# Clearing a kernel's semaphores from ScalarE beside the last store, instead of at the close of the context

## The chip, the cores and the metric

One core of a Trainium2 chip runs the kernel. In the trace each of its engines (TensorE, VectorE, ScalarE, GpSimd and SyncE) has records of its own, and these name the semaphores, which are shared counters, that an instruction waits for or counts: in the kernel before, VectorE waits for ScalarE seven times, 85.9 us in all, and ScalarE for loads five times, 34.7 us. The metric is device time in microseconds (us) of one execution. Each kernel but that of experiment 8 (fetch10) was executed several times, and the median is given with the lowest and highest run. Beside the time there is a profile of one execution; its span runs from the first to the last instruction and leaves out what comes before and after, so it is shorter than the time of the same execution: 162.18 us for 163.96 in the kernel before.

## The reference

The kernel computes log-sum-exp over the last axis of a float32 array of shape (32, 512, 1024):

```python
x_max = np.max(x, axis=axis, keepdims=True)
return (x_max.squeeze(axis) + np.log(np.sum(np.exp(x - x_max), axis=axis))).astype(np.float32)
```

That is 16,384 rows of 1,024 numbers, 67.11 MB to read and 64 KB to write. The kernel leaves out the maximum, which these inputs allow.

## The kernel before

Each of 128 partitions has 128 rows, loaded in 17 chunks into a ring of 51 rows. A chunk is a pair: its rows, and how many of them VectorE sums (ScalarE then takes only their exponentials; it sums the others itself, one row per instruction). The parts that matter here, with cuts marked:

```python
CHUNKS = [
    (4, 1), (15, 11), (16, 10), (16, 15), (16, 0), (14, 0), (12, 9), (9, 5), (7, 5), (5, 4),
    (4, 3), (3, 0), (2, 2), (2, 2), (1, 0), (1, 0), (1, 0),
]
# ...
    landed = [tc.alloc_semaphore(f"landed{i}") for i in range(len(CHUNKS))]
    act_done = tc.alloc_semaphore("act_done")
    dve_done = tc.alloc_semaphore("dve_done")
    stored = tc.alloc_semaphore("stored")
# ... loads on SyncE, exponentials on ScalarE, sums on VectorE or ScalarE ...
    take_logs(logged, NB, dves, acts)
    nc.scalar.wait_ge(act_done, acts)
    nc.scalar.dma_start(out=out_v, in_=res).then_inc(stored, 16)
    nc.gpsimd.wait_ge(stored, 16)
```

`tc` is the tile context. Semaphores taken from it are cleared when it closes. In the trace of this kernel the closing block that it writes holds a barrier over all five engines, then a clear of semaphores 99 to 118 by GpSimd (139 ns), then a second barrier. A barrier is: four engines report (each with an instruction called drain, which here adds one to semaphore 96), GpSimd takes the four reports, GpSimd releases (by semaphore 97), the four pass. From GpSimd's drain to the end of TensorE's record the first lasts 0.267 us (161.388 to 161.655) and the second 0.261 (161.918 to 162.179).

The softmax here doesn't subtract the row's maximum and nothing guards it: scores larger than these inputs give would overflow.

## Time and profile before

| | before |
|---|---|
| time, first three runs | 164.2 us (164.1 to 164.22) |
| time, all 33 runs of this study | 163.87 to 164.56 us, mean 164.16, standard deviation 0.18 |
| span of the profiled run | 162.18 us |
| issue of the store | 159.643 us |
| last of the store's 16 counts | 161.215 us |
| from that count to the end of the span | 0.964 us |

The prediction below shows the page's lines and reads them.

### The profile page before, as it was taken

Reading aid. Unit: us, or ns where it says so; the run is one execution under the profiler, and the core shown is the slowest. Engines: PE = TensorE matmul, PEld = TensorE weight load, DVE = VectorE, ACT = ScalarE, POOL = GpSimd, SP = SyncE. Lnnn points to the kernel's source line nnn. Section 1 sums busy time; section 2 is a strip of 40 time slices with the busy share of each in tenths; the row PEclk is TensorE's granted clock in tenths of the full one; section 3 lists DMA queues with packets and bytes.
Section 4 is the critical chain, followed back from the end, with each engine's and each line's share of the span. In section 5 each row is a group of like instructions: output and inputs, shape, how many; then the busy total and the mean of one; then the engine's idle time right before and its main releaser. Section 6 shows DMA issues by size and latency. Waiting matters only on the chain.

```text
span 162.2 us, 213 instructions
## 1 busy us (share of the span) xinstructions
DVE 72.9 (45%) x11; ACT 124.1 (76%) x136; POOL 0.2 (0%) x4
## 2 busy tenths in 40 slices
DVE  0030000039960799000999900000006999799591
ACT  3180006997099971999339999999999999999993
POOL 0000000000000000000000000000000000000000
DMA  6999899969969959969988999999999999999970
GB/s 263 497 485 470 349 394 517 485 291 517 485 291 517 517 259 517 517 275 501 517 368 370 424 424 432 461 497 388 436 427 399 431 400 439 420 424 414 415 318 16
DMA packets 2593, 67.18 MB, mean 414 GB/s; under 512 B 288, under 2 KB 416, under 8 KB 800
## 3 DMA queue, kind: packets, MB, share of 16 engines
q1 hardware_dynamic: 2448, 67.11, 96.4%
q10 hardware_dynamic: 144, 0.07, 0.1%
q14 instruction: 1, 0.01, 0.0%
HBM read 67.11 MB, written 0.07 MB: 414 GB/s over the span
## 4 chain that ended last, share of the span: by engine, by line
ACT 52%; DMA 38%; DVE 7%; issue 1%
DMA ring<-in_x_dram 38%; ACT ring L128 30%; ACT ring L116 22%; DVE sums L121 7%; ACT res L93 0%
## 5 line engine op out<-in xcount | busy, mean ns | idle before, releaser
L121 DVE TENSOR_REDUCE sums<-ring 128x5 f32<-128x5120 f32 (+8 forms) x11 | 72.9, 6648 | 86.0 <-ACT ring L116 85.9
L116 ACT ACTIVATE ring<-ring 128x5120 f32<-128x5120 f32 (+8 forms) x11 | 59.3, 5394 | 29.4 <-DMA ring<-in_x_dram 29.4
L128 ACT ACTIVATE ring<-ring 128x1024 f32<-128x1024 f32 x61 | 63.4, 1041 | 5.3 <-DMA ring<-in_x_dram 5.3
L128 ACT ACTIVATION_READ_ACCUMULATOR ring<-ring 128x1 f32 x61 | 11.4, 187 | 0.0
L103 ACT ACT_TABLE_LOAD x1 | 1.3, 1283 | 0.8 <-PEq L175 0.8
L93 ACT ACTIVATE res<-sums 128x67 f32<-128x67 f32 (+1 forms) x2 | 0.5, 256 | 0.1
L175 POOL MEMSET const-bfloat16-1.0<- 128x1 bf16 x1 | 0.1, 101 | 0.0
L175 POOL MEMSET const-uint8-127<- 128x1 uint8 x1 | 0.1, 101 | 0.0
L175 POOL MEMSET const-float32-0.0<- 128x1 f32 x1 | 0.1, 98 | 0.2 <-issue 0.2
L175 POOL MEMSET const-float32-1.0<- 128x1 f32 x1 | 0.1, 98 | 0.0
## 6 DMA issues: line engine op xcount, KB each, us to landing
ring<-in_x_dram SPq DMA_DIRECT2D x1, 7680.0 KB, 24.8
ring<-in_x_dram SPq DMA_DIRECT2D x1, 7168.0 KB, 36.1
ring<-in_x_dram SPq DMA_DIRECT2D x1, 6144.0 KB, 21.6
ring<-in_x_dram SPq DMA_DIRECT2D x1, 4608.0 KB, 32.1
ring<-in_x_dram SPq DMA_DIRECT2D x2, 2048.0 KB, 26.3
ring<-in_x_dram SPq DMA_DIRECT2D x1, 3584.0 KB, 40.2
ring<-in_x_dram SPq DMA_DIRECT2D x1, 2560.0 KB, 44.4
ring<-in_x_dram SPq DMA_DIRECT2D x2, 1024.0 KB, 46.0
```

The costliest lines, as they stand in the source:

```text
L93: nc.scalar.activation(out=res[:, lo:hi], in_=sums[:, lo:hi], func=Ln).then_inc(act_done, 1)
L103: nc.scalar.preload_act_table_set("natural_log_exp_and_others")
L116: nc.scalar.activation(out=ring[:, s : s + n_dve], in_=ring[:, s : s + n_dve], func=Exp).then_inc(act_done, 1)
L121: nc.vector.reduce_sum(out=sums[:, row : row + n_dve], in_=ring[:, s : s + n_dve], axis=AX).then_inc(dve_done, 1)
L128: nc.scalar.activation(out=ring[:, s + j], in_=ring[:, s + j], func=Exp, accum_out=sums[:, row + j : row + j + 1],).then_inc(act_done, 1)
L175: nc = _bacc.Bacc("TRN2", target_bir_lowering=False, num_devices=1)
```

## The change

The intent is to take the clear out of the ending. The semaphores now belong to the program and not to the context, so the context has nothing to clear; ScalarE clears them while the store is in flight, and GpSimd takes the store's own count back as it waits for it. The list of parts for the first load had one entry and goes away. Core of the diff:

```diff
-    landed = [tc.alloc_semaphore(f"landed{i}") for i in range(len(CHUNKS))]
-    act_done = tc.alloc_semaphore("act_done")
-    dve_done = tc.alloc_semaphore("dve_done")
-    stored = tc.alloc_semaphore("stored")
+    landed = [nc.alloc_semaphore(f"landed{i}") for i in range(len(CHUNKS))]
+    act_done = nc.alloc_semaphore("act_done")
+    dve_done = nc.alloc_semaphore("dve_done")
+    stored = nc.alloc_semaphore("stored")
+    used = sorted(sem.num for sem in [*landed, act_done, dve_done])
# ... the first load without its list of parts ...
     nc.scalar.dma_start(out=out_v, in_=res).then_inc(stored, 16)
+    nc.scalar.sem_clear(range(used[0], used[-1] + 1))
     nc.gpsimd.wait_ge(stored, 16)
+    nc.gpsimd.sem_inc(stored, -16)
```

More of the change, by code (lines that the diff above doesn't have):

```diff
@@ L16 @@
 LN_AT = 5
-FIRST_PARTS = [("sync", 0, 128)]
 @with_exitstack
@@ L50 @@
     res = nc.alloc_sbuf_tensor("res", [P, NB], fp32).ap()
-    landed = [tc.alloc_semaphore(f"landed{i}") for i in range(len(CHUNKS))]
-    act_done = tc.alloc_semaphore("act_done")
-    dve_done = tc.alloc_semaphore("dve_done")
-    stored = tc.alloc_semaphore("stored")
+    landed = [nc.alloc_semaphore(f"landed{i}") for i in range(len(CHUNKS))]
[3 more added lines that the diff above has]
+    used = sorted(sem.num for sem in [*landed, act_done, dve_done])
+    assert used == list(range(used[0], used[0] + len(used)))
     hook = nc.pop_inst_callback()
@@ L83, in load @@
             nc.sync.wait_ge(act_done, act_wait)
-        for engine, lo, hi in FIRST_PARTS if i == 0 else [("sync", 0, P)]:
-            getattr(nc, engine).dma_start(
-                out=ring[lo:hi, s : s + r], in_=x_v[lo:hi, row : row + r]
-            ).then_inc(landed[i], 16)
+        nc.sync.dma_start(out=ring[:, s : s + r], in_=x_v[:, row : row + r]).then_inc(
+            landed[i], 16
+        )
     def take_logs(lo, hi, dve_wait, act_wait):
@@ L113 @@
             take_logs(0, logged, *done_before[i])
-        nc.scalar.wait_ge(landed[i], 16 * (len(FIRST_PARTS) if i == 0 else 1))
+        nc.scalar.wait_ge(landed[i], 16)
         if n_dve:
```

## The prediction

> **What bounds the kernel now.** I began with the page's busy shares, its slices and the chain of waits, to see whether anything in the body can move. The kernel streams 67.11 MB from HBM through one ring of SBUF; ScalarE takes exponentials (alone or with an accumulated sum), VectorE sums part of the rows.
>
> ```profile
> DVE 72.9 (45%) x11; ACT 124.1 (76%) x136; POOL 0.2 (0%) x4
> DMA  6999899969969959969988999999999999999970
> q1 hardware_dynamic: 2448, 67.11, 96.4%
> ACT 52%; DMA 38%; DVE 7%; issue 1%
> ```
>
> The DMA row stands at 9 or 8 in most slices and the load queue holds 96.4% of the span of 16 engines: the body is bound by the transfer of x. ScalarE is full only in the second half, where it works off the chunks that have piled up in the ring. The chain alternates between loads (38%) and ScalarE (52%). GpSimd does 0.2 us of work and is in no link. The change touches neither the loads, nor an activation, nor a reduction, so the next view is the timeline of the last microseconds:
>
> ```profile
> 159.36 0.25 ACT L93 ACTIVATE res<-sums 128x61 f32<-128x61 f32 x1
> 159.64 0.37 ACTq L140 DMA_DIRECT2D out_dram<-res  x1
> ```
>
> The last logarithm ends at 159.61, the store is issued at 159.64, and the span ends at 162.18 (162.2 on the page). So 2.5 us lie after the last arithmetic. The issues view says that the 64 KB store lands 1.6 us after its issue, at 161.2. The rest, about 0.95 us, is neither compute nor data. Asking the trace for the line that closes the kernel (189, where all instructions made at the end of the context are put down) shows it:
>
> ```profile
> L189 POOLq EVENT_SEMAPHORE  x4: 17/17/17, 161.5 to 162.1; - x4
> L189 POOLq DRAIN  x3: 34/41/83, 161.4 to 161.9; - x3
> L189 POOLq COMPARE_BRANCH  x1: 33/33/33, 161.2 to 161.2; - x1
> L189 POOLq EVENT_SEMAPHORE_RANGE_CLEAR  x1: 139/139/139, 161.7 to 161.7; - x1
> ```
>
> The columns are engine, operation, count, duration in ns (least, median, most), and first and last start in us. GpSimd carries the ending. Its records in order of time, start in us and duration in ns, from the trace itself:
>
> ```
> 159.643  369  ScalarE  issue of the store
> 160.052  152  ScalarE  drain, ready for the first barrier
> 161.215       the 16th count of the store arrives
> 161.239   33  GpSimd   branch to the closing block (it holds the wait for the store)
> 161.388   41  GpSimd   drain                      }
> 161.473   17  GpSimd   takes the four arrivals    } first barrier
> 161.551   17  GpSimd   releases the four          }
> 161.604   51  TensorE  last engine passes
> 161.632   83  GpSimd   drain of the reset         } clear
> 161.744  139  GpSimd   semaphores 99 to 118 := 0  }
> 161.918   34  GpSimd   drain                      }
> 161.996   17  GpSimd   takes the four arrivals    } second barrier
> 162.074   17  GpSimd   releases the four          }
> 162.128   51  TensorE  last engine passes; the span ends at 162.179
> ```
>
> [...] the two event instructions last 17 ns each, but start 78 ns apart. So I count spacings from start to start. [...] Here, on ScalarE's queue, 64 KB at the page's mean of 414 GB/s would be 0.16 us, and 1.6 us pass[...]. That waiting time is the shadow the change wants to use. [...] semaphore 2 counts from 162.41 to 162.94, nearly all semaphores are written from 162.83 to 163.50, semaphore 2 counts again to 164.08. The profiled run took 163.96 us against a span of 162.18, so some 1.8 us are outside the kernel[...]. I take this part as unchanged.
>
> **The change part by part.**
>
> (a) The semaphores no longer belong to the tile context, so at its end the context has nothing of the kernel's to clear. Removed for certain, as I read it: the reset drain and the range clear. Without them the next GpSimd drain would start at 161.632 instead of 161.918: **0.286 us** less, all on the path, as nothing else runs then. What I must guess is whether the context then also leaves out the second barrier. That barrier exists to keep anyone from running on before the clear is done; with no clear it has no purpose. If it goes, the span ends as the last engine passes the first barrier, 161.604 + 0.051 = 161.655, and 162.179 - 161.655 = **0.524 us** go. I take this as the main case, with about 65%.
>
> (b) ScalarE clears 19 semaphores (17 landings, two counters) after issuing the store. Sized by GpSimd's clear: 139 ns, 222 with a reset drain. It starts at about 160.05, when the issue is over, so ScalarE's drain is over at about 160.204 + 0.222 = 160.43. GpSimd takes the arrivals at 161.473 in the kernel before. Over 1.0 us of slack: **0 us** on the path. Nothing still counts on these semaphores: the last wait of ScalarE asked for all activations and the one before it for all reductions.
>
> (c) GpSimd subtracts 16 as its wait is met. Before, the wait rode on the branch; now it should ride on one event instruction with the subtraction, ahead of the branch. Such an instruction costs GpSimd one spacing of 78 ns: **+0.08 us**, right on the path. If wait and subtraction were separate instructions it would be about 0.16.
>
> (d) The first load was already one transfer on SyncE; the list that could split it had one entry. Its removal changes no instruction: **0 us**.
>
> Sum of the main case: -0.524 + 0.078 = -0.45 us, 164.20 - 0.45 = 163.75 us, 0.27% less.
>
> **Rivals.** First, the second barrier stays and only the clear leaves the end: -0.286 + 0.078 = -0.21, so 163.99 us. For it: the kernel's text does not ask for a barrier less; against it: its lack of purpose. I give it 22%. Second, the clear merely changes its place, or the fixed part after the kernel absorbs the gain [...]: 164.2 to 164.3. Against it: in the trace that part starts 0.23 us after the last TensorE record, so it looks chained to the kernel's end. About 6%. Third, both barriers go and GpSimd's wait alone ends the kernel: then the path ends some 0.15 us after 161.239 + 0.078, near 161.47, and the saving is about 0.7 us, 163.5 us in all. For it: nothing but the wait is needed; against it: a context's end joins the engines whatever the semaphores. About 6%. Fourth, the clear on ScalarE becomes the wait that ends last: it would have to take over 1.0 us where GpSimd's took 0.139; 1%. No engine can become the bound, since none gets work before the store is issued.
>
> **Range and chances.** The weighted mean is near 163.8 us, and I put the prediction there, a little above the main case. The three timed runs before spread over 0.12 us; another chip or a slightly different supply of data may shift the median by as much again. All cases but the extremes lie in 163.45 to 164.15. Two per cent are 3.3 us. Everything that lies after the store's issue is 2.5 us in the trace, and most of that is the store itself, so faster by over 2% cannot come out of this; slower would need a delay of the loads for which the change has no cause. Within 2%: 0.98.
>
> **What would show it.** In the trace after: ScalarE's range clear on the line of the new clear, started near 160.05, while the store is in flight (step b); no range clear on GpSimd (a); the count of GpSimd's closing event instructions falls from 4 to 3, two for one barrier and one for the wait with the subtraction, if the second barrier went, and is 5 if it stayed; the stretch from the store's last count to the end of the span falls from 0.96 to about 0.52 us, or to about 0.76 in the first rival; start-to-start spacing of 0.08 us between the new wait and the branch (c). Up to 159.64 both traces should agree within the scatter of the loads, a few tenths of a us. The prediction is wrong if the body shifts by more than the tail saves, if the closing block keeps its shape, or if the part after the span grows as the span shrinks.

-0.524 for the clear and the second barrier, 0 for (b) and (d) and +0.078 for (c) come to -0.45 us, so to 163.75, and the mean weighted with the rivals to the 163.8 us that was predicted.

## More of the kernel before

One more line matters later, from the page's list of DMA queues (queue, kind, packets, MB, share of 16 engines' span):

```profile
q14 instruction: 1, 0.01, 0.0%
```

One transfer in the whole span does not carry data: 8 KB of instructions, at 89.05 us, 309 ns long.

## The result, and the profile after

| | before | changed |
|---|---|---|
| time, median of 6 runs each | 164.21 us (163.94 to 164.43) | 164.16 us (163.89 to 164.3) |
| span of the profiled run | 162.18 us | 162.45 us |
| sixth chunk (14 rows) landed | 100.647 us | 101.170 us |
| issue of the store | 159.643 us | 160.167 us |
| last of the store's 16 counts | 161.215 us | 161.747 us |
| from that count to the end of the span | 0.964 us | 0.701 us |

The ratio is 0.9995, with a 95% interval of 0.9981 to 1.0008. A ratio is the mean time of one kernel's runs over that of the other's runs of the same rounds, so it is not quite the ratio of the medians. In microseconds the interval says: between 0.31 less and 0.13 more. The whole kernel shows no difference; the two profiles show two, of opposite sign.

**The ending is 0.263 us shorter.** The view of the line that holds the closing block, in the changed kernel (engine, operation, count; duration in ns, least, median, most; first and last start in us):

```profile
L192 POOLq EVENT_SEMAPHORE  x4: 17/17/17, 161.9 to 162.3; - x4
L192 ACTq DRAIN  x2: 8/8/8, 160.7 to 162.2; - x2
L192 POOLq DRAIN  x2: 34/38/41, 161.9 to 162.1; - x2
```

And the views of the two new lines, ScalarE's clear and GpSimd's wait:

```profile
L142 ACTq EVENT_SEMAPHORE_RANGE_CLEAR  x1: 119/119/119, 160.6 to 160.6; - x1
L144 POOLq EVENT_SEMAPHORE  x1: 17/17/17, 161.8 to 161.8; - x1
```

Read the counts. GpSimd's closing block still has four event instructions, two per barrier, and the new wait is a fifth on a line of its own. So **both barriers stayed**; the reset drain, the range clear and the branch that carried the wait are gone from GpSimd. Following GpSimd's records from start to start shows where the time went:

| stretch (us) | before | changed |
|---|---|---|
| last count of the store, to GpSimd going on | 0.024 | 0.025 |
| GpSimd's wait, to its first drain | 0.149 | 0.080 |
| first drain, to the first release | 0.163 | 0.164 |
| first release, to the taking of the second four reports | 0.445 | 0.249 |
| that, to the second release | 0.078 | 0.078 |
| second release, to the end of the span | 0.105 | 0.105 |
| sum | 0.964 | 0.701 |

Two rows changed, by 0.069 and 0.196.

**The body was 0.52 us longer.** The chain of waits in order of time (start, duration, what), before:

```profile
47.15 36.52 DMA ring<-in_x_dram
83.69 10.55 ACT ring L128 x21
...
100.46 0.26 ACT res L93
100.72 14.60 ACT ring L128 x28
```

and in the changed kernel:

```profile
64.66 36.51 DMA ring<-in_x_dram
101.17 0.02 issue
101.19 14.65 ACT ring L127 x28
```

Before, ScalarE reached the sixth chunk just as it had landed, at 100.65. In the changed kernel the chunk landed at 101.17, ScalarE waited for it, and from there ScalarE works without a gap to the end: its first instruction on the sixth chunk starts 0.52 us later and the store is issued 0.52 us later. Nothing that the change touches runs between 2 and 160 us, so the cause is elsewhere. The 16 counts of that load tell more. The trace has 16 counts for every load, and from 30 to 156 us, gaps of up to 25 ns aside, 16 packets of x are under way at a time, but for the stretch named below; I read each count as the part of one of 16 DMA engines that has landed. From the trace, the time between the 15th and the 16th count, in ns:

```
                     before   changed
fifth chunk              27        27
sixth chunk              47       501
seventh chunk            47       480
last chunk               25       452
```

In the changed kernel, by that reading, **one of 16 engines fell half a microsecond behind between the fifth and the sixth chunk** and stayed behind to the end. Within that time, at 89.49 us, falls the one transfer of instructions (before: 89.05). It lasts 309 ns in both traces; for 303 of them (before: 284) 15 packets of x are under way and not 16, and one of the packets that start as it ends takes 2.446 us (before: 2.379), where the median of its size is 2.116. Whether that transfer is able to do it is tested below.

### The profile page after: what moved, and what is told of

It reads as the page before. It is cut to its first block, busy times and chain, and to the rows that moved or that the text cites. A ratio compares the mean times of both kernels' runs of the same rounds, so it can differ in the third digit from the quotient of the medians.

```text
span 162.4 us, 212 instructions
## 1 busy us (share of the span) xinstructions
DVE 72.9 (45%) x11; ACT 124.1 (76%) x136; POOL 0.2 (0%) x4
## 4 chain that ended last, share of the span: by engine, by line
DMA 49%; ACT 42%; DVE 7%; issue 0%; SPq 0%
DMA ring<-in_x_dram 49%; ACT ring L115 22%; ACT ring L127 20%; DVE sums L120 7%; SPq L84 0%; ACT res L92 0%
```

## The experiments

Two questions: is the gain of 0.26 us real outside the profile, and made of the parts that I read; and what hides it in the whole kernel? My theory T says that the ending is shorter in earnest, and the scatter of the loads hides it. Rival R1 says that the fixed part after the kernel takes the gain back. Rival R2 keeps the terms of the prediction.

To take the loads' scatter away I cut the body to its first chunk. The result is then wrong; the ending is the same. The edit that all "short" kernels share:

```diff
+    nc.vector.memset(sums[:, CHUNKS[0][0] :], 1.0).then_inc(dve_done, 1)
+    dves += 1
-    for i, (r, n_dve) in enumerate(CHUNKS):
+    for i, (r, n_dve) in enumerate(CHUNKS[:1]):
```

**1. short_old: the kernel before, cut.** No further edit.

> The kernel before with its body cut to the first chunk of four rows, so that the long stream of loads and its scatter are gone (wrong result on purpose, same outputs and same ending). It is the base for the other short kernels. Theory T (the ending really became shorter, and the scatter of the loads hides it): span about 15 us, and from the store's last count to the end of the span 0.96 us as in the full kernel before. Runs should lie within 0.1 us of each other, where the full kernel scattered by 0.5 us.

Measured: 16.27 us (16.25 to 16.33, 4 runs). The span was 14.55 us and the ending 0.964 us, as in the whole kernel. The scatter is 0.08 us.

**2. short_new: the changed kernel, cut.** No further edit.

> The changed kernel with the same cut. T: 0.26 us less than short_old in the time as well as in the ending (0.70 us from the store's last count to the end of the span). Rival R1 (the fixed part after the kernel takes the gain back): ending 0.26 us shorter, time the same. Rival R2 (the terms of the prediction's first rival: clear 0.286 less, one event instruction 0.078 more): 0.21 us less.

Measured: 15.98 us (15.95 to 16.04, 4 runs), 0.29 us less by the medians, with no overlap of the runs. The ending is 0.701 us, again as in the whole kernel. Semaphore 2, which counts only outside the span (18 times ahead of it and 18 behind in both whole kernels) and so belongs to the part around the kernel, counts for the last time 1.904 us after the end of the span in both kernels. So R1 falls: nothing is taken back. The gain is real, and 0.26 us in size; R2's 0.21 is less than either reading.

**3. short_one_barrier: the second barrier taken out.** After the context has closed, the program's last block is cut to its first barrier:

```diff
+    last = nc.main_func.blocks[-1]
+    kept = []
+    for ins in last.instructions:
+        name = str(ins.engine)
+        seen = sum(1 for k in kept if k.engine == ins.engine)
+        if seen < (3 if "Pool" in name or "SP" in name else 2):
+            kept.append(ins)
+    last.instructions = kept
```

> short_new with the second barrier taken out of the closing block. If the prediction's main case only failed because that barrier stays, this is what it foresaw: T expects about 0.33 us less than short_new (the spacing of the two releases in the changed kernel, 162.016 to 162.343), 0.59 us less than short_old; the ending 0.37 us. R1: no change in time.

The view of the closing line in this kernel:

```profile
L194 POOLq EVENT_SEMAPHORE  x2: 17/17/17, 13.7 to 13.8; - x2
L194 POOLq DRAIN  x1: 41/41/41, 13.6 to 13.6; - x1
```

Measured: 15.72 us (15.68 to 15.78, 4 runs), 0.26 less than short_new and 0.55 less than short_old. The ending is 0.372 us, 0.329 less, so 0.07 us of it did not reach the time; of these the trace shows 0.04, as the part after the span took 1.945 us instead of 1.904. This is the saving on which the prediction's main case had counted: the barrier is worth that much, but the change does not remove it.

**4. short_poolclear: the clear on GpSimd, ahead of the first barrier.**

```diff
-    nc.scalar.sem_clear(range(used[0], used[-1] + 1))
     nc.gpsimd.sem_inc(stored, -16)
+    nc.gpsimd.sem_clear(range(used[0], used[-1] + 1))
```

> short_new with the clear moved from ScalarE to GpSimd, behind its wait for the store and ahead of the first barrier. T: the clear is now on the path with nothing to cover it, so 0.14 to 0.2 us more than short_new (139 ns for the clear and up to 83 for a drain). If the clear's place did not matter: the same as short_new.

Measured: 16.16 us (16.09 to 16.2, 5 runs), 0.18 more than short_new. In the trace the clear starts at 13.658 and the next drain at 13.825, 0.167 us, and no other drain comes with it. With nothing beside it the clear costs its whole length; so the change does save it by putting it in the shadow of the store.

**5. short_clear16: ScalarE's clear sixteen times.**

```diff
+    for _ in range(16):
-    nc.scalar.sem_clear(range(used[0], used[-1] + 1))
+        nc.scalar.sem_clear(range(used[0], used[-1] + 1))
```

> short_new with the clear on ScalarE sixteen times over. T: one clear costs ScalarE 0.158 us from start to start, and its readiness for the barrier has 1.19 us of room (12.455 to 13.650 in short_new), so seven more would cost nothing and fifteen more (2.37 us) cost 1.18: about 17.15 us. If the clear were on the path already: +2.37 us. If ScalarE's clear slowed the store: the store's 1.58 us from issue to last count grow.

The view of ScalarE's clears:

```profile
L145 ACTq EVENT_SEMAPHORE_RANGE_CLEAR  x16: 115/115/119, 12.3 to 14.4; - x16
```

Measured: 16.91 us (16.9 to 16.98, 5 runs), 0.93 more than short_new. Clears that follow each other start 0.140 us apart, not 0.158, so ScalarE's report came 2.13 us later in the trace (14.586 for 12.455, of bodies that agree within 0.03 us). GpSimd was ready at 13.67 and took the reports at 14.610. So 1.19 us of the 2.13 were hidden and 0.94 showed. That is the room behind one clear, which step (b) of the prediction had put at over 1.0 us. The first clear itself does not even delay the report: from the issue of the store to ScalarE's report it is 0.568 us in short_old and 0.571 in short_new, as the drain behind the issue takes 152 ns without the clear and 8 ns behind it. The store took 1.58 us from issue to last count in both, so the clears do not disturb it.

**6. short_takeback, twice: GpSimd's taking back alone.** The semaphores stay with the context and the clear stays in the ending:

```diff
     nc.gpsimd.wait_ge(stored, 16)
+    nc.gpsimd.sem_inc(stored, -16)
```

> short_old with one line added: GpSimd takes 16 off the store's count as its wait is met; the semaphores stay with the context, so the clear stays at the end. It is step (c) of the prediction alone. The prediction said +0.08 us. Theory T, read from the changed kernel's trace (wait to the next drain 80 ns, where the branch that carried the wait took 149): 0.07 us less than short_old (16.27 us).

Measured in the first batch: 16.31 us (16.25 to 16.34, 4 runs), but short_old was of another batch. So I repeated both on one chip:

> The short form of the kernel before once more, beside the next run on the same chip, because the first comparison of the two was made across two batches and the times scatter by 0.05 us. 16.27 us as the first time, within 0.06.

> The short form of the kernel before with the taking back of the store's count alone, again. T (wait off the branch, 69 ns less in the trace): 0.07 us less than short_old_b. The prediction's step (c): 0.08 us more. If the first comparison holds (16.31 against 16.27): 0.04 more, and the trace's saving would be given back outside the span.

Measured: short_old_b 16.3 us (16.25 to 16.34, 4 runs), short_takeback_b 16.22 us (16.14 to 16.36, 4 runs). Over both batches, eight runs each, the means are 16.289 and 16.266: 0.02 less, with a 95% interval of about 0.06 either way. **The time does not settle this step.** The traces do so for the span: in both profiles of short_takeback the ending is 0.896 us against 0.964 in both of short_old. GpSimd's wait to its first drain takes 81 ns, where the branch that carries the wait takes 148 or 149. So the new instruction does not cost 78 ns; it saves 68: with the wait on an event instruction the trace has no record of a branch, and the next drain starts 81 ns later. Why the branch with the wait takes longer is not shown.

**7. full_one_barrier: the whole changed kernel with the edit of experiment 3.**

> The changed kernel, whole, with the second barrier taken out. T: 0.55 us less than the kernel before (0.29 and 0.26 from the short kernels), a ratio of 0.9967, the scatter of the loads (some 0.25 us either way) on top. R1: ratio 1.000.

Measured: 163.55 us (163.46 to 163.64, 5 runs) against 164.18 us (163.94 to 164.4, 9 runs) of the kernel before, correct results, ratio 0.9965 with an interval of 0.9952 to 0.9977. This is 0.57 us less, where the short kernels said 0.55. It beats both kernels: its highest run lies below the lowest of the kernel before. A gain of twice the change's size is seen through the scatter; the change alone is not.

That the scatter is all that hid the change is not shown. The six runs of the changed kernel have a mean of 164.11 us, 0.05 below the mean of the 33 runs of the kernel before, where T asks for 0.26 to 0.29. With a standard deviation of 0.18 and independent runs, my estimate of the standard error of that difference is 0.08, so their bodies would have to be late by chance by 2.6 to 3 of these. The interval of the paired runs (0.31 less to 0.13 more) just holds T. Against a lasting delay that the change brings speaks the present kernel, which has the same body and shows none.

**8. fetch10: ten more transfers of instructions.** Whether a transfer of instructions can put one DMA engine behind, I tested by multiplying it. GpSimd, which is idle in the body (0.2 us of work, at its start), gets 1,280 semaphore instructions that do nothing:

```diff
+    spare = nc.alloc_semaphore("spare")
     ...
     logged = 0
+    for _ in range(640):
+        nc.gpsimd.sem_inc(spare, 1)
+        nc.gpsimd.sem_inc(spare, -1)
```

> The changed kernel with 1,280 extra semaphore instructions on GpSimd, which has nothing else to do, to bring in about ten more 8 KB transfers of instructions. Theory F (the half microsecond by which the body of the profiled changed kernel was later came from one of 16 DMA engines that served the one instruction transfer at 89.5 us between two packets of x and stayed behind to the end): with ten of them, one or a few engines fall behind by 0.3 us each time, and the body ends 0.3 us (if they are spread over the engines) to 3 us (if one engine gets all) later. Rival: such transfers fit in between, the lag was chance, and the body ends as before, at 159.6 to 160.2.

The queue view, and lines of the chain of waits:

```profile
q14 instruction: 11, 0.09, 0.1%
```

```profile
66.69 39.92 DMA ring<-in_x_dram
106.61 0.02 issue
106.63 14.65 ACT ring L131 x28
```

Measured: 169.61 us (one run, of unknown state), 5.45 us more than the changed kernel's median. There were eleven transfers, the added ones about every 10.3 us. GpSimd's instructions start 78 ns apart, with a pause of 0.37 us (0.43 the first time) once in every 128, ten times, so that is one transfer for 128 of them. From the trace, the time between the 15th and the 16th count of the chunks' landings, in ns, with the transfers up to then:

```
second chunk, 26 us      718     2 transfers
third chunk,  47 us    1,987     4
fourth chunk, 68 us    3,262     6
fifth chunk,  88 us    4,162     8
sixth chunk, 107 us    5,461    11
last chunk,  164 us    5,346    11
```

The lag grows in step with the transfers, by some 0.5 us for each, and stays when they end. Only the 16th count is late, so, if each count is one engine's, all, or nearly all, of the added transfers fell on one engine. The sixth chunk landed at 106.61 instead of 101.17, ScalarE began it 5.44 us later, and the store was issued 5.38 us later. Theory F holds in its strongest form, beyond the 3 us that I had put as its most. What it shows is that with eleven such transfers the last count is behind by 5.46 us at the sixth chunk, half a microsecond for each, and that the lag stays (5.35 at the last chunk). That the one transfer did so in the profiled run of the changed kernel is by the fit of time and size (27 ns before it, 501 after it; 15 packets under way while it runs), not by an engine's number, which the records do not have. In the kernel before, with its transfer at 89.05 us, no count fell out of line. The counts show why. Here are all 16 of the fifth and of the sixth chunk, sorted, in ns from the fifth's eighth count, and the sixth's laid over them:

```
fifth  -339 -279 -266 -184 -116  -45  -43    0   21   54   74   88  114  178  303  330
sixth  -323      -257 -185 -114  -52  -38    0   21   54   68   89  108  163  301  320  367
```

If one engine moved, 15 counts agree within 16 ns and one went from second to last, back by 0.65 us. The kernel of experiment 7, with its transfer at 88.89 us, shows the same at the same place: 15 within 26 ns, one back by 0.69. So an engine was probably held up there too (in the kernel before the trace shows the 15 packets and the long one), but one that was ahead of the others, and the body was not late. By this reading the pair of profiles differs in which engine was held up; the records have no engine's number, so it is argued and not shown.

One rival is left by fetch10 alone: that the added semaphore instructions, and not the transfers which they bring, hold the engine up. The next pair of runs speaks against it.

**9. few_act and few_act_one_barrier: a try to be rid of that transfer.** It missed.

```diff
-    (4, 1), (15, 11), (16, 10), (16, 15), (16, 0), (14, 0), (12, 9), (9, 5), (7, 5), (5, 4),
+    (4, 1), (15, 11), (16, 10), (16, 15), (16, 16), (14, 6), (12, 9), (9, 5), (7, 5), (5, 4),
-LN_AT = 5
+LN_AT = 6
```

> The changed kernel with 42 fewer instructions on ScalarE: the fifth chunk is summed wholly by VectorE, six rows of the sixth too, and the first logarithm is taken one chunk later. Theory F (the one instruction transfer near 89 us holds up one DMA engine by some 0.6 us, and that engine then lands its part of every later chunk last): ScalarE's stream is short enough for no such transfer, the last load lands 0.2 to 0.5 us earlier, the time is 163.6 to 163.9 us and the runs lie closer together. Rival: the transfer is not what sets the body's end, and the time stays at 164.1. If the transfer still comes, the run decides nothing.

> few_act with the second barrier taken out. If the two are independent: 0.26 us less than few_act (short_new to short_one_barrier), so 163.3 to 163.6 us under theory F, and the fastest of all; 163.85 under its rival.

Lines of few_act's waits and queues:

```profile
ACT res L92 <- DVE sums L120: 7.1, 1, 7.1
```

```profile
q14 instruction: 1, 0.01, 0.0%
```

Measured: 169.93 us (169.83 to 169.98, 4 runs) and 169.65 us (169.43 to 169.96, 5 runs). The transfer still came, now at 125.56 us, and my new division made ScalarE wait 7.1 us for VectorE before the first logarithm, more than the 5.8 us by which the kernel is slower. As the expectation said, the time of a run with the transfer decides nothing about F. That it moved with ScalarE's work speaks for its being ScalarE's. Its counts bear on F, as there are no added instructions here. From the first to the last count the sixth chunk, which no transfer precedes now, takes 0.635 us (the fifth 0.673), and no count falls behind. The seventh takes 0.664, and the eighth, the first to land after the transfer, 1.153 (the ninth 1.002). In few_act_one_barrier, with the transfer at 125.04 us, it is 0.693 for the sixth, 0.691 for the seventh and 0.930 for the eighth (0.787 for the ninth). The step moved with the transfer. The other thing to be had from the pair is that the second barrier's removal gave 0.28 us between the medians, near the 0.26 of the short kernels.

## Why the prediction was right or wrong

The class was right: within 2%, because everything after the store's issue is 2.5 us and most of that is the store (1.57 us from issue to last count). The size was not: 163.8 us was predicted, 164.16 measured, 0.01 above the upper end of the stretch in which the prediction put all cases but the extremes (164.15). Two of the signs that it had named came true against it: GpSimd has five event instructions and not three, and in the pair of profiles the body moved by more (0.52 us) than the ending saved (0.26). Step by step:

- **(a), the choice of the main case, failed.** I gave 65% to the second barrier going away with the clear. It stayed: GpSimd has four closing event instructions and the wait. The argument was that the barrier has no purpose without a clear; what the barrier is for was my guess, which no trace shows, and what a program's author finds purposeless, a context may write all the same. The size that I gave to that case, 0.524 us for clear and barrier together, was sound: in the traces short_old's ending less short_one_barrier's is 0.592, of which 0.068 belong to step (c).
- **(a), the clear itself: the mechanism was right, the term mis-sized.** I put 0.286 us for drain and clear, "all on the path, as nothing else runs then". Measured: 0.196. Something else did run: after the first release the four engines were on their way to the second barrier. Before, their last report arrived at 161.776, and GpSimd, still clearing, took the four at 161.996, 0.22 us later. In the changed kernel GpSimd is ready earlier, and the last report arrives at 162.241; GpSimd takes them at 162.265. A new wait of 0.09 us, for TensorE's report, took that much of the gain away.
- **(b) was right.** ScalarE's clear is hidden: behind it 1.19 us of room are left, and it does not delay ScalarE's report (0.571 us after the issue, 0.568 without it).
- **(c) had the wrong sign.** I added 0.078 us for one more instruction, and left the branch at its old cost. The traces show 0.069 less: from the branch that carries the wait to GpSimd's first drain it is 0.149 us, from the event instruction that carries it 0.080, with no record of a branch between. The clock outside the span did not settle it.
- **(d) was right**: the loads are the same instructions in the same order.
- **The rivals.** The first, with the second barrier kept, is what came true; I had given it 22%. Its two terms were each off, by -0.09 and +0.15 us of gain, so that their sum, 0.21, came near the 0.26 of the trace (0.29 of the short kernels' times) by luck. The second, that the fixed part takes the gain back, is refuted for the change by the 1.904 us in both short kernels.
- **The scatter was too small.** I took 0.12 us from three runs. The kernel's 33 runs spread over 0.69 us. I had asked what could shift the body and found no cause in the change, which was correct; I did not ask how much the body moves by itself. In the pair of profiles it moved by 0.52 us and hid the ending's 0.26. Whether chance alone did so in the other runs is open, as said under experiment 7.

## What to carry to other kernels

Work that is moved off a barrier's path is worth its length only up to the next arrival at that barrier (here 0.196 us of the 0.286 that I had counted): look at what the other engines do meanwhile before you count it in full. When a gain at the end of a kernel is smaller than the scatter of its body (here 0.26 against 0.69 us), cut the body away and measure the ending by itself; here 16 us kernels resolved what 164 us kernels could not. And check in the program that a thing without a purpose is really gone before you count its saving.
